# Low parts of 24 U chunks made ahead and kept in DRAM, and the rows of h2 and x1 in buffers of their own

## Chip, cores and metric

The kernel runs on one core of one Trainium2 chip. The metric is the device time of one execution in microseconds (us), as the median of several runs; a smaller number is better.

## What is computed

One decoder block on 512 tokens of width 1024, in float32. The first sub-layer mixes tokens (a gated MLP over positions, a windowed attention, two sigmoid branch gates, an output projection, a layer norm). The second, which takes two thirds of the time here, retrieves single-neuron experts:

```python
q = (xb @ w_pq).reshape(-1, PEER_HEADS, PEER_QDIM)          # xb: h2, the modulated x1
s1, s2 = keys1 . q1, keys2 . q2                             # 128 scores for each half of a head
v1, i1 = lax.top_k(s1, 16); v2, i2 = lax.top_k(s2, 16)
sc, ci = lax.top_k(v1[:, None] + v2[None, :], 16)           # 16 of 16384 experts, for each of 8 heads
g = jax.nn.softmax(sc)
act = gelu(einsum('thkd,td->thk', peer_u[e], xb))
out = einsum('thk,thkd->td', g * act, peer_v[e])
x = layer_norm(ALPHA * x + (1.0 + gt2) * out, ln2_g, ln2_b)
```

## The kernel before

**Numbers.** A float32 product is made of three TensorE products: each operand is split into a rounded high part (`hi`, a copy on ACT, ScalarE) and a low part (`lo = raw - hi`, on DVE, VectorE, or on POOL, GpSimd), and `mm3` (lines 57 to 65) runs hi x hi, hi x lo and lo x hi. A weight chunk of 128 x 1024 so costs one load of 512 KB, one ACT copy, one subtraction and the products.

**The first sub-layer** is staged as: modulation (`mod_chunk`, line 144: one 512 KB load `wa` and one DVE operation each), queries and attention, the gated MLP (`w_u`, then the position mixing into `aT`), then gate b and projection b in eight iterations (lines 341 to 350; each also does four `mod_chunk`), then gate a and projection a in eight iterations (lines 372 to 384), then the output projection and the layer norm (lines 387 to 429), which leave `xhat` (x1 before its gain and offset) and `h2T` (h2, transposed and split). `load_split` (line 112) loads and splits a weight chunk; its raw tiles and those of `mod_chunk` share one tag `raw` with 4 buffers.

**The experts.** The first three blocks of 128 tokens (384 tokens) are computed densely: all 16384 experts in 128 chunks of 128, U chunk (`h2T` by `peer_u`, 24 products of 384 columns) and V chunk (18 products of 512 columns into six accumulators). The last block of 128 tokens is computed by gathering: 128 rows of `peer_u` and 128 of `peer_v` for each token, through indirect DMAs on POOL's queue into the tag `rows` (4 buffers), each reduced by one DVE operation (`gather`, line 663). The order of stages:

- queries and scores (16 chunks of w_pq), while DVE finds the top 16s; U chunks follow while that lasts. In these stages the low parts are made by POOL (`last["pool"]`, line 455).
- spread (`spread`, line 606): the gates of 384 tokens are written out over all 16384 experts, in 24 groups of 16 tokens: for each, four DVE operations make one-hot tiles `oh`, TensorE multiplies them (32 products of 128 columns, f16), ACT copies the result to `stg`, and SP (SyncE) stores it to `Gd` in DRAM. Beside it run U chunks whose low parts DVE makes; 21 of them (NRES) stay in SBUF (`U_resident`, line 695) and are multiplied by the gates there; the others store their activations in `Ad`.
- rows (`rows_x1`, line 484): `h2n` (h2 of the last block, in natural layout, for the gather) and x1 out of `xhat`, in place, with rows loaded into the tag `raw` of `load_split2` (4 buffers).
- three more U chunks (VDLY), the 21 V chunks of the resident ones, then U and V chunks in pairs with the gather beside them ("pairs"), at last the V chunks of those whose activations went to `Ad` ("tail", loads `ar`), and the final layer norm.

**What sets the order.** The program is written as one sequence. Work that is to run beside other work is a list of generators, `bg`; `pump(us)` advances it by so many estimated microseconds per chunk. A planner then orders the instructions of each engine at compile time: an instruction goes where its engine is free and its operands are ready by the planner's own times, and among several that are ready the earlier one of the program goes first. On the chip each engine runs its instructions in that order, and one that waits holds up all behind it. `behind(a, b)` puts a after b on their engine.

## Time and profile before

| | us |
|---|---|
| median of 3 runs | 1731.55 (1729.62 to 1737.84) |
| the profiled execution | 1727.13 |
| its span, first to last instruction | 1725.4 |
| TensorE busy in it | 1667.5 (97%) |
| VectorE busy | 1346.7 (78%) |
| ScalarE busy | 685.6 (40%) |
| GpSimd busy | 474.2 (27%) |

A matmul counts as busy from its start to its modelled end, and several are in flight, so a busy TensorE need not be one at its full rate: the number of matmuls in a stretch tells more. In a table of stretches the granted clock (PEclk) is 1.00 at 2.4 GHz and 0.50 at 1.2 GHz; a value between is a mean of both over the stretch. The DMA share is the mean busy share of the core's 16 DMA engines. A row of such a table gives: stretch (us from the span's start), its length, then busy us and number of instructions (x) of PE (TensorE), PEld (its weight loads), DVE, ACT and POOL, then PEclk, DMA share and GB/s.

### The profile page before, as it was taken

The page shows a single profiled execution, that of the slowest core. Times are in us where ns is not written, and L with a number is a line of the kernel's source. Part 1 is how long each engine was busy: PE and PEld are TensorE (multiplying, and loading weights), DVE is VectorE, ACT ScalarE, POOL GpSimd, SP SyncE. Part 2 cuts the span into 40 slices and gives each one's busy share as a digit, 9 for nine tenths or more (in the row PEclk, how much of TensorE's full clock was granted, in tenths as well). Part 3 has the DMA queues.
Part 4 walks back from the last instruction along what each step waited for, and adds up shares of the span by engine and source line. Part 5 has one row for each costly group of instructions (what it writes and reads, how often), then busy time and mean ns, then how long its engine had stood idle before and what let it go on. Part 6 is the DMA issues. An engine that isn't in the chain of part 4 may idle for free.

```text
span 1725.4 us, 23595 instructions
## 1 busy us (share of the span) xinstructions
PE 1667.5 (97%) x8658; PEld 1440.2 (83%) x8658; DVE 1346.7 (78%) x2510; ACT 685.6 (40%) x1095; POOL 474.2 (27%) x333
## 2 busy tenths in 40 slices
PE   6999999999999999999999999999999999999997
PEld 3865778788788999999987789999999999988776
DVE  6467785554559999999988887878787888787687
ACT  3467632233333333455443233333333333343333
POOL 2000000000043455300014544434444545541102
PEclk9999999999999999999999999999999999999999
DMA  7502267642232355566599999999899899899973
GB/s 270 200 1 74 98 198 256 210 144 95 86 120 85 112 173 174 209 218 226 203 316 365 373 328 333 325 339 348 306 336 334 326 336 341 303 372 312 306 235 106
DMA packets 158695, 409.52 MB, mean 237 GB/s; under 512 B 19217, under 2 KB 66097, under 8 KB 158322
## 3 DMA queue, kind: packets, MB, share of 16 engines
q1 hardware_dynamic: 121186, 273.47, 46.2%
q0 software_dynamic: 36960, 134.50, 21.6%
q8 instruction: 68, 1.11, 0.3%
q14 instruction: 49, 0.40, 0.1%
q10 hardware_dynamic: 432, 0.04, 0.0%
HBM read 376.88 MB, written 30.82 MB: 236 GB/s over the span
## 4 chain that ended last, share of the span: by engine, by line
PE 52%; DVE 20%; issue 5%; DMA 4%; POOL 2%; ACT 1%; SPq 0%; DVEq 0%; POOLq 0%; ACTq 0%
PE acc L802 7%; PE acc L803 7%; PE acc L799 7%; PE psU L64 6%; PE psU L62 6%; PE psU L63 6%; POOL ru L669 2%; DMA ar<-Ad 2%; DMA wa<-in_w_ada_dram 2%; DVE oh L634 1%; DVE loU L458 1%; DVE oh L637 1%; DVE oh L633 1%; DVE oh L636 1%; DVE loV L458 1%
## 5 line engine op out<-in xcount | busy, mean ns | idle before, releaser
L62 PE MATMUL psU<-h2Thi,hiU 128*128 128x384 f32 x1008 | 340.9, 338 | 5.4 <-ACT hiU L450 3.7
L64 PE MATMUL psU<-h2Thi,loU 128*128 128x384 f32 x1008 | 340.4, 338 | 3.5 <-DVE loU L458 3.4
L63 PE MATMUL psU<-h2Tlo,hiU 128*128 128x384 f32 x1008 | 339.2, 337 | 0.0
L802 PE MATMUL acc<-loV,wh 128*128 128x512 f32 x768 | 301.5, 393 | 5.5 <-DVE loV L458 5.5
L803 PE MATMUL acc<-hiV,wl 128*128 128x512 f32 x768 | 300.5, 391 | 0.3 <-DVE wl L785 0.3
L799 PE MATMUL acc<-hiV,wh 128*128 128x512 f32 x768 | 298.8, 389 | 1.7 <-ACT wh L784 1.7
L669 POOL DMA_INDIRECT ru<-in_peer_u_dram,idx x128 | 157.2, 1228 | 368.6 <-DVE ru L673 351.5
L682 POOL DMA_INDIRECT rv<-in_peer_v_dram,idx x128 | 174.1, 1360 | 248.3 <-DVE facc L688 221.4
L458 DVE TENSOR_TENSOR loV<-rawV,hiV 128x1024 fp32r<-128x1024 f32 x128 | 156.3, 1222 | 90.3 <-ACT hiV L450 90.2
L450 ACT ACTIVATE hiV<-rawV 128x1024 fp32r<-128x1024 f32 x128 | 135.1, 1056 | 224.3 <-PE psU L63 188.6
L450 ACT ACTIVATE hiU<-rawU 128x1024 fp32r<-128x1024 f32 x126 | 133.9, 1062 | 216.6 <-POOL loU L456 68.0
L62 PEld LDWEIGHTS psU<-h2Thi,hiU 128*128 128x128 f32 x1008 | 190.5, 189 | 8.8 <-ACT hiU L450 3.9
L64 PEld LDWEIGHTS psU<-h2Thi,loU 128*128 128x128 f32 x1008 | 190.3, 189 | 5.3 <-DVE loU L458 5.2
L63 PEld LDWEIGHTS psU<-h2Tlo,hiU 128*128 128x128 f32 x1008 | 190.6, 189 | 2.6
L802 PEld LDWEIGHTS acc<-loV,wh 128*128 128x128 f32 x768 | 144.1, 188 | 39.5 <-DVE loV L458 10.9
L673 DVE SCALAR_TENSOR_TENSOR ru<-ru,h2n 128x1024 f32<-128x1024 f32 x128 | 154.4, 1220 | 24.3 <-DMA ru<-in_peer_u_dram,idx 24.1
L803 PEld LDWEIGHTS acc<-hiV,wl 128*128 128x128 f32 x768 | 144.1, 188 | 30.8 <-DVE wl L785 1.0
L799 PEld LDWEIGHTS acc<-hiV,wh 128*128 128x128 f32 x768 | 144.2, 188 | 30.5 <-ACT wh L784 2.0
L688 DVE SCALAR_TENSOR_TENSOR facc<-rv,wg,facc 128x1024 f32<-128x1024 f32 x126 | 159.4, 1279 | 11.4 <-DMA rv<-in_peer_v_dram,idx 11.4
L784 ACT ACTIVATE wh<-wf 128x384 fp32r<-128x384 f32 x107 | 56.1, 525 | 182.1 <-DVE wf L780 106.2
L456 POOL TENSOR_TENSOR lopq<-rawpq,hipq 128x1024 fp32r<-128x1024 f32 x16 | 39.0, 2445 | 322.2 <-ACT hipq L450 322.2
L458 DVE TENSOR_TENSOR loU<-rawU,hiU 128x1024 fp32r<-128x1024 f32 x96 | 116.9, 1218 | 2.8 <-ACT hiU L450 2.8
(629 smaller groups left out, 2929.4 us busy)
## 6 DMA issues: line engine op xcount, KB each, us to landing
rawU<-in_uT_dram SPq DMA_DIRECT2D x128, 512.0 KB, 4.2
rawV<-in_peer_v_dram SPq DMA_DIRECT2D x128, 512.0 KB, 6.2
wa<-in_w_ada_dram SPq DMA_DIRECT2D x48, 512.0 KB, 4.2
G<-Gd SPq DMA_DIRECT2D x11, 1536.0 KB, 14.8
Gd<-stg SPq DMA_DIRECT2D x24, 600.0 KB, 4.3
rawpq<-in_w_pq_dram SPq DMA_DIRECT2D x16, 512.0 KB, 3.6
Ad<-act SPq DMA_DIRECT2D x39, 192.0 KB, 2.2
ar<-Ad SPq DMA_DIRECT2D x9, 768.0 KB, 8.5
```

What stands on the lines that cost most here:

```text
L62: nc.tensor.matmul(ps, l.hi, r.hi, start=(i == 0), stop=False)
L63: nc.tensor.matmul(ps, l.hi, r.lo, start=False, stop=False)
L64: last = nc.tensor.matmul(ps, l.lo, r.hi, start=False, stop=(i == n - 1))
L450: h = nc.scalar.activation(hi, raw, AF.Copy)
L458: last["dve"] = nc.vector.tensor_sub(lo, raw, hi.bitcast(F32))
L669: d = nc.gpsimd.indirect_dma_start(out=rows, out_offset=None, in_=I["peer_u"], in_offset=bass.IndirectOffsetOnAxis(ap=idx[:, s:s + 1], axi ...
L673: paced(nc.vector.scalar_tensor_tensor(rows, rows, 1.0, h2n, op0=ALU.mult, op1=ALU.mult, accum_out=wg[:, s:s + 1]))
L682: nc.gpsimd.indirect_dma_start(out=rows, out_offset=None, in_=I["peer_v"], in_offset=bass.IndirectOffsetOnAxis(ap=idx[:, s:s + 1], axis=0))
L688: paced(nc.vector.scalar_tensor_tensor(fa, rows, wg[:, s:s + 1], fa, op0=ALU.mult, op1=ALU.add))
L799: m = nc.tensor.matmul(acc, l.hi, r.hi, start=st, stop=False)
L802: nc.tensor.matmul(acc, l.hi, r.lo, start=False, stop=False)
L803: nc.tensor.matmul(acc, l.lo, r.hi, start=False, stop=sp_)
```

## The change

Three parts:

1. The low parts of the last 24 U chunks (104 to 127) are made during the first sub-layer, in 48 halves of 128 x 512. For each half, POOL's queue loads 256 KB of `uT` into one of two buffers (tag `ht`, free by then), ACT copies it to a PSUM bank rounded (`hi`), DVE writes raw - hi in place, and POOL's queue stores it to a new DRAM tile `LoD`. The steps are written into the iterations of gate b (three in each) and of gate a (three in each); the first load is put behind the mask of the position mixing on POOL.
2. These 24 chunks are the first taken when the spread starts (`ready`): the 21 resident ones and three more. Their low part is loaded from `LoD` by SP (512 KB each), and DVE makes none. The U chunks 32 to 52, which were resident before, come among the pairs.
3. `rows_x1` is split: `rows_h2` is the first background work of the query stage and takes its rows into the tag `rows` of the gather; x1 is queued as background work at the start of the pairs, its two rows one after the other in the tag `facc1`.

```diff
+NPS = 24
+    LoD = dram.tile([NPS, P, D], F32, name="LoD")
+        def presplit():
+            raws = {}
+
+            def load(k):
+                raws[k] = wp.tile([P, S], F32, name=f"praw{k}", tag="ht", bufs=2)
+                d = nc.gpsimd.dma_start(raws[k], I["uT"][NCH - NPS + k // 2, :, (k % 2) * S:(k % 2 + 1) * S])
+                if k == 0:
+                    behind(d, mask)
+            load(0)
+            load(1)
+            for k in range(2 * NPS):
+                yield
+                hi = bank("po", 1, f"phi{k}").bitcast(F32R)
+                nc.scalar.activation(hi, raws[k], AF.Copy)
+                lo = raws[k].bitcast(F32R)
+                nc.vector.tensor_sub(lo, raws[k], hi.bitcast(F32))
+                nc.gpsimd.dma_start(LoD[k // 2, :, (k % 2) * S:(k % 2 + 1) * S], raws[k])
+                if k + 2 < 2 * NPS:
+                    load(k + 2)
+        ps_steps = presplit()
...
             for i in range(16 + 4 * j, 20 + 4 * j):
                 mod_chunk(i)
+                if i % 4 < 3:
+                    presplit_some(1)
...
             ps = proj_T(load_split(I["w_gate"][j], f"ga{j}"), hT, f"psga{j}")
+            presplit_some(2)
...
             ps = proj_T(load_split(I["w_pa"][j], f"pa{j}"), aT, f"pspa{j}")
+            presplit_some(1)
...
         wo[1] = load_split_wide(I["w_out"][1], "wo1", ("G", "H"))
+        presplit_some(100)
...
-    def load_split2(src, nm, pool=None):
+    def load_split2(src, nm, pool=None, low=None):
...
-        if last.get("pool"):
+        if low is not None:
+            nc.sync.dma_start(lo.bitcast(F32), low)
+        elif last.get("pool"):
...
-    def rows_x1():
-        g2r, b2r = raw_row("g2r"), raw_row("b2r")
+    def rows_h2():
+        g2r, b2r = (gat.tile([P, D], F32, name=nm, tag="rows", bufs=4) for nm in ("g2r", "b2r"))
...
-        g1, b1 = raw_row("g1"), raw_row("b1")
-        nc.sync.dma_start(g1, I["ln1r"][0].partition_broadcast(P))
-        nc.sync.dma_start(b1, I["ln1r"][1].partition_broadcast(P))
-        for t in range(NT):
-            nc.vector.tensor_mul(xhat[:, t, :], xhat[:, t, :], g1)
-            nc.vector.tensor_add(xhat[:, t, :], xhat[:, t, :], b1)
-            yield 2.4
+
+    def rows_x1():
+        for i, op in enumerate((ALU.mult, ALU.add)):
+            row = gat.tile([P, D], F32, name=f"ln1_{i}", tag="facc1", bufs=1)
+            nc.sync.dma_start(row, I["ln1r"][i].partition_broadcast(P))
+            for t in range(NT):
+                nc.vector.tensor_tensor(xhat[:, t, :], xhat[:, t, :], row, op=op)
+                yield 1.2
...
-        w = load_split2(I["uT"][i], f"U{i}")
+        w = load_split2(I["uT"][i], f"U{i}", low=LoD[i - NCH + NPS] if i >= NCH - NPS else None)
...
+    bg.append(rows_h2())
     qt = query(0, 0)
...
-        res["first"] = cur[0] + 1
+        res["first"] = NCH - NPS
...
-    bg += [topk_last(), softmax(), end_topk(), spread(), end_spread(), rows_x1()]
+    bg += [topk_last(), softmax(), end_topk(), spread(), end_spread()]
...
-    i = NPRE + 1
+    todo, ready = list(range(NPRE + 1, NCH - NPS)), list(range(NCH - NPS, NCH))
     while not done or len(res["ids"]) < NRES:
-        cur[0] = i
+        i = (ready if res and ready else todo).pop(0)
...
     for _ in range(VDLY):
+        i = (ready or todo).pop(0)
...
-    uvruns = runs(range(i, NCH))
+    todo += ready
+    uvruns = runs(todo)
...
     pend = None
+    bg.append(rows_x1())
...
-    for run in runs(spilled):
+    for run in runs(sorted(spilled)):
```

## Rows read from the trace of the kernel before

**Rows 1.** The page: each engine's busy us, share of the span, instructions.
```profile
PE 1667.5 (97%) x8658; PEld 1440.2 (83%) x8658; DVE 1346.7 (78%) x2510; ACT 685.6 (40%) x1095; POOL 474.2 (27%) x333
```

**Rows 2.** Table of stretches (columns above): spread, resident V chunks, pairs.
```profile
750.00:800.00 50.00, 49.76 (x449) 48.19 (x448) 50.00 (x63) 26.94 (x55) 0.00 (x0) 1.00 0.67 235
900.00:950.00 50.00, 48.09 (x206) 37.79 (x205) 40.45 (x61) 16.74 (x23) 22.50 (x19) 1.00 1.02 372
1050.00:1100.00 50.00, 50.00 (x254) 45.54 (x254) 40.75 (x61) 18.17 (x24) 21.93 (x19) 1.00 0.97 343
```

**Rows 3.** Timeline of TensorE in the spread: start us, us, engine, line, operation.
```profile
774.97 0.33 PE L62 MATMUL psU<-h2Thi,hiU 128*128 128x384 f32 x1
775.84 0.34 PE L64 MATMUL psU<-h2Thi,loU 128*128 128x384 f32 x1
776.21 0.23 PE L645 MATMUL psg<-oh,oh 128*128 128x128 f16 x1
778.01 0.22 PE L646 MATMUL psg<-oh,oh 128*128 128x128 f16 x1
```

**Rows 4.** Groups by line, 710 to 868 us: count, busy us, mean ns, idle before.
```profile
L62 PE MATMUL psU<-h2Thi,hiU 128*128 128x384 f32 x199 | 68.6, 345 | 1.7 <-ACT act L716 1.0 <-ACT act L706 0.7
L645 PE MATMUL psg<-oh,oh 128*128 128x128 f16 x368 | 44.9, 219 | 1.6 <-DVE oh L637 1.4
L458 DVE TENSOR_TENSOR loU<-rawU,hiU 128x1024 fp32r<-128x1024 f32 x25 | 30.3, 1214 | 0.7 <-ACT hiU L450 0.7
```

**Rows 5.** Stretches of 10 us: the spread's start, and the rows after its end.
```profile
710.00:720.00 10.00, 7.68 (x36) 7.17 (x35) 9.93 (x13) 4.41 (x7) 5.17 (x4) 0.83 0.86 318
870.00:880.00 10.00, 6.06 (x33) 5.38 (x31) 8.87 (x9) 5.49 (x10) 0.00 (x0) 0.67 0.84 285
```

**Rows 6.** Timelines of DVE and ACT at the spread's end.
```profile
867.61 1.21 DVE L489 TENSOR_TENSOR h2n<-xhat,g2r 128x1024 f32<-128x1024 f32 x1
...
873.57 1.06 ACT L450 ACTIVATE hiU<-rawU 128x1024 fp32r<-128x1024 f32 x1 [1.85 <-DMA rawU<-in_uT_dram]
```

**Rows 7.** Stretches of 10 us in gate b (the first has the stage's start).
```profile
260.00:270.00 10.00, 10.00 (x32) 7.99 (x33) 5.02 (x10) 1.34 (x2) 0.00 (x0) 0.71 0.79 262
290.00:300.00 10.00, 10.00 (x46) 8.29 (x45) 7.68 (x11) 2.56 (x3) 0.00 (x0) 1.00 0.68 231
```

**Rows 8.** Waits, whole span: total us, times, longest us.
```profile
DVE wf L780 <- DMA ar<-Ad: 32.9, 8, 5.4
DVE wa L147 <- DMA wa<-in_w_ada_dram: 32.0, 21, 3.3
```

**Rows 9.** DMA issues by line: queue, count, KB each, median us to landing.
```profile
rawU<-in_uT_dram SPq DMA_DIRECT2D x128, 512.0 KB, 4.2
...
Gd<-stg SPq DMA_DIRECT2D x24, 256.0 KB, 3.0
...
xr<-in_x_dram SPq DMA_DIRECT2D x8, 256.0 KB, 2.7
```

**Rows 10.** Timelines of POOL, ACT and DVE: two iterations of gate a, operations like presplit's.
```profile
57.98 0.76 POOL L206 DMA_DIRECT2D kd<-kd  x1 [23.53 <-ACT kd L204]
...
396.35 0.58 ACT L377 ACTIVATE ga<-psga 128x512 f32<-128x512 f32 x1
...
407.23 0.58 ACT L377 ACTIVATE ga<-psga 128x512 f32<-128x512 f32 x1
...
401.07 0.69 DVE L380 TENSOR_TENSOR mt<-pspa,ga 128x512 f32<-128x512 f32 x1 [3.37 <-PE pspa L64]
```

**Rows 11.** The mask on POOL (timeline), and the output projection's products (view of one tile).
```profile
203.39 1.59 POOL L314 TENSOR_SCALAR_AFFINE_SELECT wst<-wst 128x1024 f32<-128x1024 f32 x1 [109.39 <-DMA wst<-in_w_sp_dram]
...
L62 PE MATMUL pso<-wwhiwo,mThi x64: 389/389/395, 422.6 to 467.5; 128*128 128x512 f32 x64
```

**Rows 12.** Timeline of DVE at the start of the top 16s.
```profile
495.85 0.49 DVE L535 MAX8 v0h__3571<-sall 128x8 f32<-128x128 f32 x2 [11.94 <-ACT sall L532]
...
498.91 0.28 DVE L535 MAX8 v0l__5222<-sall 128x8 f32<-128x128 f32 x1
```

More of the change, by code (lines that the diff above doesn't have):

```diff
@@ L65, in mm3, with behind @@
         return last
+    def behind(ins, other):
+        tc.add_manual_dep(ins.ins, other.ins.name,
+                          mybir.DependencyInfo(mybir.DependencyClass.NoSync, mybir.DependencyReason.DATA))
     const = ctx.enter_context(tc.tile_pool(name="const", bufs=1, reuse_waits="tile"))
@@ L313, in block_kernel @@
         nc.sync.dma_start(wst, I["w_sp"])
-        nc.gpsimd.affine_select(wst, wst, pattern=[[0, 8], [1, P]], compare_op=ALU.is_ge, fill=0.0, base=0,
+        mask = nc.gpsimd.affine_select(wst, wst, pattern=[[0, 8], [1, P]], compare_op=ALU.is_ge, fill=0.0, base=0,
                                 channel_multiplier=-1)
@@ L338, in block_kernel, with presplit_some @@
         sp_.close()
+        def presplit():
[17 more added lines that the diff above has]
+        ps_steps = presplit()
+        def presplit_some(n):
+            for _ in range(n):
+                next(ps_steps, None)
         gp = fr.enter_context(tc.tile_pool(name="gp", bufs=1, reuse_waits="tile"))
@@ L435, in block_kernel @@
     last = {}
-    def behind(ins, other):
-        tc.add_manual_dep(ins.ins, other.ins.name,
-                          mybir.DependencyInfo(mybir.DependencyClass.NoSync, mybir.DependencyReason.DATA))
     def paced(ins):
         behind(ins, last["dve"])
-    def load_split2(src, nm, pool=None):
+    def load_split2(src, nm, pool=None, low=None):
         raw = pw.tile([P, NK * P], F32, name=f"raw{nm}", tag="raw", bufs=4)
@@ L477, in pump @@
                 bg.pop(0)
-    def raw_row(nm):
-        return pw.tile([P, D], F32, name=nm, tag="raw", bufs=4)
     h2n = gat.tile([P, D], F32, name="h2n", tag="facc0", bufs=1)
-    def rows_x1():
-        g2r, b2r = raw_row("g2r"), raw_row("b2r")
+    def rows_h2():
+        g2r, b2r = (gat.tile([P, D], F32, name=nm, tag="rows", bufs=4) for nm in ("g2r", "b2r"))
         nc.sync.dma_start(g2r, rowsD[2].partition_broadcast(P))
@@ L710, in U_chunk @@
     def U_chunk(i, keep_act):
-        w = load_split2(I["uT"][i], f"U{i}")
+        w = load_split2(I["uT"][i], f"U{i}", low=LoD[i - NCH + NPS] if i >= NCH - NPS else None)
         ps = pu.tile([P, SD], F32, name=f"psU{i}", tag="mm", bufs=2)
@@ L816, in block_kernel @@
     res = {}
-    cur = [NPRE]
     def end_topk():
@@ L867, in block_kernel @@
             pump(GPUMP if res else UPUMP + 1.2 * bool(last.get("pool")))
-        i += 1
     open_v()
     for _ in range(VDLY):
+        i = (ready or todo).pop(0)
         U_chunk(i, False)
@@ L873, in block_kernel @@
         pump(2.7)
-        i += 1
-    uvruns = runs(range(i, NCH))
+    todo += ready
+    uvruns = runs(todo)
     for n, j in enumerate(res["ids"]):
```

## The prediction

> **What bounds the kernel now.** I read the page first: TensorE is busy for 97% of the span [rows 1], so only a stretch in which TensorE falls short of its own rate can give time back. The table of stretches shows where that is, once matmuls are counted and not busy time. The rate comes from the timeline of the spread: two U products five apart start 0.87 us apart, 0.174 us each; 32 one-hot products start within 1.80 us, 0.058 us each [rows 3]. Two iterations of gate a, 48 products of 512 columns each, lie 10.88 us apart [rows 10], 0.227 us a product. A pair of a U and a V chunk then needs 24 x 0.174 + 18 x 0.227 = 8.26 us for 42 products, 254 in 50 us, and 254 is what the pairs reach [rows 2]. So the pairs are bound by TensorE and gain nothing from a freer DVE.
>
> The spread is not: DVE is busy there without a gap, 50.00 of 50 us [rows 2]. From 710 to 868 us it ran, among others, 25 subtractions loU of 1.21 us [rows 4]. But TensorE is close behind. It ran 595 U products there (199 of the kind shown, 198 of each of the two others) and 736 one-hot products (368 of each of two kinds) [rows 4]: 595 x 0.174 + 736 x 0.058 = 146 us of work in 158 us. **Only 12 us are lost in the spread**, 10 - 36 x 0.174 = 4 of them in its first 10 us, where the clock was at 1.2 GHz for a part (0.83), and the rest in small waits behind DVE. After its end come another 10 - 33 x 0.174 = 4 us, at a clock of 0.67 [rows 5]: the rows of h2 and x1 stand in DVE's order there (first at 867.61), their loads have taken raw buffers, and ACT waits for the next rawU until 873.57 [rows 6].
>
> **What the change removes.** First, 24 of the 25 subtractions of the spread, 24 x 1.21 = 29 us of DVE [rows 4]. DVE would need 158 - 29 = 129 us, TensorE 146: TensorE is late next. The pairs show that TensorE can run at its rate beside a busy DVE, but the start of the spread stays a chain through DVE (last top 16, softmax, first one-hots), so of its 4 us I leave 3: the spread gives **-9 us**, not -29. Ends: 0, if another wait takes its place, and -12, TensorE at its rate throughout.
> Second, ten row operations (1.21 us each [rows 6], 12 us of DVE) and four loads of 512 KB leave the end of the spread. The 4 us there shrink to what another boundary costs; I take **-4 us** (ends -5 and -2).
>
> **What it moves.** The h2 rows (two loads on SP, two DVE operations) go to the start of the query stage. There DVE has an idle stretch of 11.94 us before the first top 16 [rows 12], so 2.4 us are hidden; without that cover they would delay the top 16s by 2.4 us, during which DVE is full. The planner does pull work forward: an operation of the last block's top 16 (v0l), written after all heads, runs at 498.91, three microseconds after the first [rows 12]. The eight x1 operations depend on nothing but xhat and a free facc1 buffer, so they can go into the same gap; if they stay in the pairs, they meet a DVE that is busy 40.75 of 50 us [rows 2], 1.5 us free per pair, and need six or seven pairs. The second row's load waits on SP for the four multiplications, with rawU and rawV behind it; a raw buffer or two cover that. I take 0 for both, ends 0 and +4. By its pacing (2.4 estimated us less for the top 16s) one more U chunk falls into the stage before the spread: 40 chunks spilled instead of 39, 67 pairs instead of 68. TensorE's work is the same; the spilled list is now 0 to 36 and 125 to 127, six runs instead of five, 11 ar loads instead of 10. The waits for ar are 32.9 us in 8 [rows 8], 4 us each, some of it behind DVE's backlog: **+1.5 us** (ends 0 and +4).
>
> **What it adds in the spread.** 24 loads of 512 KB on SP, 12.6 MB, at 372 GB/s of full rate [rows 2] 34 us of all 16 engines. The spread's share of 0.67 [rows 2] is some 106 of 158 us; with the loads 140 of 149 us, 0.94. It fits, barely. A low part's buffer comes free when TensorE is done with the third chunk before, so its load has two chunks of 6 us each for a landing that now takes 4.2 [rows 9] and will take longer. **+2 us** (ends 0 and +9, the whole gain of the spread).
>
> **What it adds in the first sub-layer** is the term I know least, since no row shows a load, a split and a store in two buffers. One step by the nearest rows: ACT 0.58, DVE 0.69, an issue on POOL 0.76 [rows 10], the store landing 3.0, another issue 0.76, the load landing 2.7 [rows 9]: 8.5 us for a buffer, 4.2 us per step with two buffers; with 0.1 us for each of four handoffs (an estimate), 4.4. 48 steps need 211 us. The steps are written three to an iteration of 10.9 us: one in 3.6 us, 174 us in all. But the loads can start behind the mask, whose operation ends at 205 us, and the output projection's last products start at 467.5 [rows 11]: 262 us. So it fits if the planner spreads the steps by their real length. ACT and DVE have the time (28 and 33 us in all). DMA has not, in gate b: share 0.68 to 0.79 [rows 7]; DVE waits there for wa loads, 32.0 us in all, 21 times [rows 8], and the iterations just keep TensorE's rate (46 products begun or running in 10 us). Eight iterations take 87 us; 87 / 4.4 = 20 steps fall into gate b, 20 x 0.524 MB = 10.5 MB or 28 us at 372 GB/s on top of some 0.7 x 87 = 61: 89 of 87, saturated. A wa that lands 1 us later, with six raw loads per iteration through four buffers that are each used for about 7 us, costs 0 to 2 us of an iteration, and where TensorE falls idle the clock follows, as after 260 us, where it was 0.71 and 32 products were done instead of 46 [rows 7]. **+6 us**, between 0 (hidden by the slack) and +37 (below).
> The Trainium skill (DMA: Bandwidth & Descriptors, "Anatomy of one DMA") puts a DMA of this queue at 2.0 us plus its bytes over 436 GB/s. By that page 256 KB would take 2.6 us, and a step by estimate 4.2 instead of 4.4; the same formula would put rawU's 512 KB at 3.2 us where the row shows 4.2, so under load it is too low here, and I keep the rows.
>
> **The sum.** -9 - 4 + 0 + 1.5 + 2 + 6 = -3.5 us. The profiled execution took 1727.13 us, 1.7 above its span; it is 4.4 us under the median of the runs, which I take as the base: 1731.5 - 3.5 = **1728 us**. Half a per cent is 8.7 us, about what a measurement of this kernel can tell from no change.
>
> **The rivals.** (1) *The steps are hidden.* If the planner keeps wa ahead and the steps fill idle time, the front costs nothing and the spread's loads little: -12 - 5 + 1.5 = -15.5 at best, with the middle values -9 - 4 + 1.5 = -11.5, **1720 us**. For it: ACT's and DVE's idle time and the empty POOL queue in these stages. Against: the DMA share in gate b.
> (2) *The two buffers pace the front; slower than before.* If the planner takes a step for shorter than the chip does, it places the steps as densely as written, one in 3.6 us; each one then holds ACT, and all splits behind it, until its load has landed. It decides when a step really takes over 3.6 us where it was planned so: 3 x 4.4 = 13.2 us an iteration instead of 10.9, 16 x 2.3 = +37 us, so 1731.5 - 13 + 1.5 + 2 + 37 = **1759 us**; if only gate a, or half of the steps, are so, 1741. For it: in-order engines, and DVE's waits for wa, which show the order already runs into DMAs that land late. Against: a plan that starts at 205 us has 262 / 48 = 5.5 us for each step, and DVE and ACT have idle time in gate b (7.68 and 2.56 of 10 us busy [rows 7]).
> (3) *The spread becomes bound by DMA.* At a share of 0.94 the low parts land late and the 9 us do not come: 1731.5 - 4 + 1.5 + 6 = **1735 us**. For it: the resident V chunks, where the share is 1.02 and 206 products of mostly 512 columns (220 at the rate) are done in 50 us [rows 2]. Against: nearly everything in the spread is issued one or two chunks ahead.
> That the subtractions do not go away can't be: 24 chunks take their low part by load, and 25 run in the spread.
>
> **How the numbers follow.** The forecast with its neighbourhood, rival 3 included: 0.43, all within 8.7 us. Rival 1 and combinations beyond 8.7 us faster: 0.32. Rival 2, in whole or in part: 0.25. The range for 8 in 10 goes from 1716 (rival 1 at its best) to 1752 (two thirds of rival 2's price); beyond are the rest of rival 2 and a little below. By the same cases: faster by over 0.5% 0.32, within 0.5% 0.43, slower by over 0.5% 0.25.
>
> **What would show it.** In the profile after: no loU on DVE between the start of the spread and its end, DVE busy below 90% there, and some 146 us of products in about 150 us; the products per 10 us around the end of the spread at 55 or more, with the clock at 1.00. In the first sub-layer: 45 to 46 products per 10 us from 270 to 420 us if the steps are hidden, 38 and ACT waiting for the praw loads if rival 2 holds. The query stage starts later by what the front costs. For rival 3: TensorE or its weight loads waiting for a DMA of LoD, share above 0.95. The forecast is wrong if the output projection starts more than 15 us later than before (422.6 us [rows 11]), or if the spread does not get shorter by at least 5 us.

## The result, and the profile after

The changed kernel takes **1772.82 us** (median of 4, 1771.38 to 1777.24) against 1732.26 us (median of 4 runs of the kernel before): a ratio of **1.0244 [1.0223, 1.0265]** on record (these two medians by themselves give 1.0234): slower by a little over 2%. That is 45 us above the forecast and 21 us beyond the upper end of its range. All readings below are made between the two profiled executions, of 1773.86 and 1727.13 us: 46.7 us apart, 6 more than the medians, since the profiled execution of the kernel before is 5 us under its median.

The busy line of the page after, which answers to [rows 1]:

```profile
PE 1683.5 (95%) x8658; PEld 1446.0 (82%) x8658; DVE 1358.3 (77%) x2533; ACT 710.5 (40%) x1143; POOL 533.4 (30%) x430
```

TensorE has the same 8658 products; its busy time rose by 16 us, since single matmuls count as busy for longer (for pso up to 795 ns in the view below, 395 before; the median is 389 in both). Where the time went is read from the first products of four stages. The view of one tile, kernel after (line, engine, operation, count: min/median/max ns, first to last start in us); the line for pso answers to [rows 11]:

```profile
L63 PE MATMUL psgb<-hThi,whigb x64: 389/389/501, 234.2 to 356.2; 128*128 128x512 f32 x64
L63 PE MATMUL psga<-hThi,whiga x64: 387/389/499, 365.3 to 468.4; 128*128 128x512 f32 x64
L63 PE MATMUL pso<-wwhiwo,mThi x64: 389/389/795, 474.5 to 526.5; 128*128 128x512 f32 x64
L63 PE MATMUL psq<-h2Thi,hipq x128: 389/389/502, 541.3 to 640.8; 128*128 128x512 f32 x128
```

Gate b starts at 234 us, as before; then the stages fall back, to 52 us at the output projection and 58.5 us at the queries. Read in the same way for every kernel of this study (us from the first product of a stage to the first of the next; spread from its first to its last one-hot product, V from the first V product to the last):

| kernel | gate b | gate a | output projection, norm | queries and U | spread | to first V | V |
|---|---|---|---|---|---|---|---|
| before | 102.5 | 87.2 | 60.2 | 241.2 | 146.7 | 19.4 | 824.3 |
| **after** | **131.1** | **109.2** | **66.8** | **243.7** | **142.3** | **12.6** | **821.1** |
| e1, no steps after the first two | 94.3 | 87.2 | 61.2 | 248.2 | 142.2 | 12.7 | 819.2 |
| e2, transfers only | 125.9 | 87.2 | 61.2 | 248.4 | 142.2 | 12.7 | 822.1 |
| e3, engines' work only | 96.0 | 87.2 | 59.7 | 245.1 | 142.2 | 12.7 | 820.9 |
| e4, four buffers | 132.4 | 113.2 | 61.3 | 245.3 | 142.3 | 12.6 | 821.2 |
| e12, transfers of half the bytes | 118.1 | 87.2 | 62.4 | 248.5 | 142.2 | 12.6 | 822.9 |
| e14, transfers only, fifth raw buffer | 109.9 | 87.1 | 62.5 | 245.7 | 142.2 | 12.6 | 822.0 |
| e6, rows only | 102.0 | 87.1 | 59.8 | 247.8 | 146.9 | 12.4 | 821.0 |
| e5, 24 paced steps | 109.1 | 87.2 | 59.7 | 247.3 | 144.7 | 12.6 | 822.8 |
| e9, 24 paced steps after gate b | 102.9 | 87.2 | 67.5 | 246.4 | 144.6 | 12.7 | 818.3 |
| e10, 16 steps in gate a | 103.9 | 87.1 | 61.3 | 247.3 | 145.2 | 12.5 | 822.5 |
| e11, 2 early steps and 16 in gate a | 96.5 | 87.2 | 61.2 | 247.3 | 145.2 | 12.5 | 824.0 |
| e13, 2 early steps only | 94.3 | 87.1 | 59.7 | 248.5 | 148.4 | 12.4 | 825.5 |

One row against another: gate b +28.6, gate a +22.0, output projection +6.6, with 1.3 us ahead of gate b **+58.5 us in the front**; behind it +2.5 -4.4 -6.8 -3.2 = **-11.9 us**. V alone varies by some 3 us between kernels that have the same work there, so single differences of that size mean nothing. A row is one execution of its kernel, and not always a typical one: those of e4, e12 and e14 took 6.5, 6.2 and 4.5 us more than the medians of their kernels, those of e6 and of the kernel before 4.0 and 5.1 less.

What is late in gate a is plain in ScalarE's timeline. Kernel after, 13 us of gate a, about one iteration (start us, us, engine, line, operation, and in brackets the idle time before and what ended it):

```profile
386.90 0.60 ACT L361 ACTIVATE phi<-praw 128x512 fp32r<-128x512 f32 x1 [3.99 <-DMA praw<-in_uT_dram]
...
390.12 0.60 ACT L361 ACTIVATE phi<-praw 128x512 fp32r<-128x512 f32 x1 [2.06 <-DMA praw<-in_uT_dram]
390.65 1.04 ACT L126 ACTIVATE whiga<-rawga 128x1024 fp32r<-128x1024 f32 x1
391.60 0.58 ACT L413 ACTIVATE ga<-psga 128x512 f32<-128x512 f32 x1
396.55 0.60 ACT L361 ACTIVATE phi<-praw 128x512 fp32r<-128x512 f32 x1 [4.36 <-DMA praw<-in_uT_dram]
399.33 0.60 ACT L361 ACTIVATE phi<-praw 128x512 fp32r<-128x512 f32 x1 [2.18 <-DMA praw<-in_uT_dram]
399.86 1.04 ACT L126 ACTIVATE whipa<-rawpa 128x1024 fp32r<-128x1024 f32 x1
```

The phi copies stand in ScalarE's order ahead of whiga and whipa, the high parts of the next weights; each waits 2 to 4 us for its load, and the weights wait with it. The table of waits, kernel after, of the whole span (engine, line, what it waited for: us in total, times, longest us):

```profile
ACT phi L361 <- DMA praw<-in_uT_dram: 149.5, 41, 8.1
POOL LoD L364 <- DVE praw L363: 123.7, 39, 21.9
...
DVE praw L363 <- ACT phi L361: 98.7, 38, 5.6
POOL praw L353 <- DMA LoD<-praw: 97.4, 33, 7.1
```

It is a ring in which each waits for the next: the copy for the load, the subtraction for the copy, POOL's store for the subtraction, POOL's next load for the landing of the store. And TensorE at the end of it, in the waits of 234 to 365 us and of 365 to 474 us:

```profile
PE pspb L63 <- ACT whipb L126: 13.1, 4, 4.5
```
```profile
PE pspa L63 <- ACT whipa L126: 5.5, 3, 2.6
PE pspa L65 <- DVE wlopa L127: 5.4, 4, 2.1
```

Such a wait can be charged twice, where the granted clock falls with it: 18 products at 0.88, 18 and 26 at 0.66. It does not always (27 products at 1.00). Stretches of gate b and gate a, kernel after, which answer to [rows 7] (us, then busy time and count of PE, PEld, DVE, ACT and POOL, granted clock, DMA share, GB/s):

```profile
260.00:270.00 10.00, 10.00 (x46) 8.29 (x45) 9.55 (x15) 2.46 (x4) 1.09 (x2) 1.00 0.93 295
...
300.00:310.00 10.00, 5.29 (x18) 3.57 (x17) 4.62 (x6) 1.58 (x2) 1.81 (x4) 0.88 0.71 248
...
340.00:350.00 10.00, 6.67 (x18) 4.86 (x19) 5.65 (x8) 3.64 (x5) 2.19 (x4) 0.66 0.64 222
...
420.00:430.00 10.00, 6.96 (x27) 4.65 (x26) 4.10 (x7) 3.67 (x7) 2.20 (x4) 1.00 0.58 201
430.00:440.00 10.00, 8.87 (x26) 7.10 (x27) 4.22 (x6) 3.39 (x6) 2.20 (x4) 0.66 0.60 214
```

18 products in 10 us where 46 are the rate. In the two worst of these stretches the DMA share is 0.64 and 0.71: the transfers are being waited for, and the engines that make them are not full.

The spread went as hoped. Groups of the kernel after between its first and its last one-hot product, which answer to [rows 4], and two stretches in it, which answer to [rows 2]:

```profile
L63 PE MATMUL psU<-h2Thi,hiU 128*128 128x384 f32 x182 | 62.5, 343 | 0.0
...
L493 DVE TENSOR_TENSOR loU<-rawU,hiU 128x1024 fp32r<-128x1024 f32 x4 | 4.9, 1220 | 1.9 <-ACT hiU L483 1.9
```
```profile
800.00:850.00 50.00, 49.80 (x436) 48.48 (x435) 42.53 (x58) 27.38 (x57) 0.00 (x0) 1.00 0.88 312
850.00:900.00 50.00, 49.72 (x455) 48.26 (x455) 41.22 (x54) 28.28 (x58) 0.00 (x0) 1.00 0.84 306
```

4 subtractions are left (from 909.5 us on, in its last 18 us), DVE is busy for 82 to 85% of these stretches instead of all the time, and TensorE for 49.7 to 49.8 of 50 us. 547 U products (182 or 183 of each kind) at 0.174 and 768 one-hot products at 0.058 us make 139.7 us of work in 142.3. Around the spread's end 97 and 60 products per 10 us are done at a clock of 1.00 (920 to 940 us), where it was 33 at 0.67.

### The profile page after: what moved, and what is told of

It reads as the page before. It is cut to its first block, busy times and chain, and to the rows that moved or that the text cites. A ratio compares the mean times of both kernels' runs of the same rounds, so it can differ in the third digit from the quotient of the medians.

```text
span 1772.1 us, 23951 instructions
## 1 busy us (share of the span) xinstructions
PE 1683.5 (95%) x8658; PEld 1446.0 (82%) x8658; DVE 1358.3 (77%) x2533; ACT 710.5 (40%) x1143; POOL 533.4 (30%) x430
## 3 DMA queue, kind: packets, MB, share of 16 engines
q1 hardware_dynamic: 128018, 286.45, 46.7%
## 4 chain that ended last, share of the span: by engine, by line
PE 50%; DVE 18%; issue 15%; DMA 12%; POOL 3%; ACT 1%; SPq 0%; DVEq 0%; POOLq 0%; ACTq 0%
PE acc L835 8%; PE acc L836 8%; PE acc L832 7%; PE psU L65 5%; PE psU L63 5%; PE psU L64 5%; DMA praw<-in_uT_dram 5%; DMA LoD<-praw 3%; POOL ru L702 2%; DMA ar<-Ad 1%; PE pss L253 1%; DMA ru<-in_peer_u_dram,idx 1%; PE psgv L63 1%; PE psgv L65 1%; PE psgv L64 1%
## 5 line engine op out<-in xcount | busy, mean ns | idle before, releaser
L363 DVE TENSOR_TENSOR praw<-praw,phi 128x512 fp32r<-128x512 f32 x48 | 32.9, 685 | 98.8 <-ACT phi L361 98.7
L491 POOL TENSOR_TENSOR loU<-rawU,hiU 128x1024 fp32r<-128x1024 f32 x31 | 76.6, 2470 | 61.4 <-ACT hiU L483 61.4
```

## The experiments

Three theories were to be told apart. **A**: the steps' transfers take DMA time from the weights of gate b. **B**: a step holds ScalarE's in-order queue until its load has landed. **C** (rival 2 of the prediction in its narrow form): the two buffers set the pace, and more of them would help. The recorded expectations have letters of their own: A1 in them is B here, A2 is A, A3 that the engines' own work costs time; from e4 on C there is A and B together, and D is C here.

**e1, no steps after the first two.** Against the change (all 24 chunks then load the first one's low part, so the loads of the spread stay):

```diff
-            for k in range(2 * NPS):
+            for k in range(2):
-                if k + 2 < 2 * NPS:
+                if k + 2 < 2:
...
-        w = load_split2(I["uT"][i], f"U{i}", low=LoD[i - NCH + NPS] if i >= NCH - NPS else None)
+        w = load_split2(I["uT"][i], f"U{i}", low=LoD[0] if i >= NCH - NPS else None)
```

> The change without 46 of the 48 presplit steps: only halves 0 and 1 are loaded, split and stored, and the 24 ready chunks all load this one low part (so 23 chunks are multiplied by the low part of another: that part of the computation is left out). All of the query, spread and pairs stages is as in the change. Theory A (the steps in the gate stages cost all that was lost, the later stages gain): the output projection starts within 3 us of 422.6 us and the time is 14 us below before, 1714 to 1722 us. Theory B (the later stages lose too, by loads of low parts that share the DMA engines): 1728 to 1735 us.

Measured 1710.91 us, 0.9877 [0.986, 0.9893], 3 us under the expected range. So the 46 later steps cost 62 us, all of it in the front: gate b 94.3 instead of 131.1, gate a 87.2 instead of 109.2. It also did something that no theory had: its gate b is 8 us shorter than that of the kernel before (e13 below).

**e2, transfers only**, and **e3, engines' work only.** e2 leaves the copy and the subtraction out of each step, so that raw halves are stored:

```diff
-                hi = bank("po", 1, f"phi{k}").bitcast(F32R)
-                nc.scalar.activation(hi, raws[k], AF.Copy)
-                lo = raws[k].bitcast(F32R)
-                nc.vector.tensor_sub(lo, raws[k], hi.bitcast(F32))
```

e3 keeps these and leaves out the loads and stores of all steps but the first two:

```diff
+                raws[k] = raws.get(k - 2)
+                if k >= 2:
+                    return
...
-                nc.gpsimd.dma_start(LoD[k // 2, :, (k % 2) * S:(k % 2 + 1) * S], raws[k])
+                if k < 2:
+                    nc.gpsimd.dma_start(LoD[k // 2, :, (k % 2) * S:(k % 2 + 1) * S], raws[k])
```

> All 48 steps of the change with their loads and stores in the same two buffers on POOL's queue, but without the ACT copy and the DVE subtraction: what is stored as the low part is the raw chunk (the low parts of 24 chunks are left out). Theory A1 (ACT and DVE wait in order for each half's load; the traffic does not matter): the gate stages keep TensorE's rate, the output projection starts at 423 to 430 us, time 1716 to 1724. Theory A2 (DMA bandwidth in gate b: wa, gb and pb land late because of 25 MB more): the output projection still starts at 450 us or later, time above 1745.

> All 48 ACT copies and DVE subtractions of the change at their places, on two buffers that are loaded and stored once each (the low parts of 23 chunks are left out), without the other 46 loads and 46 stores. Theory A1 (the wait for transfers is the cost, ACT's 28 us and DVE's 33 us are hidden): output projection at 423 to 430 us, time 1716 to 1726. Theory A3 (ACT and DVE are late by their own work, as DVE is full before gate b): output projection 10 to 30 us later than before, time 1730 to 1750.

Measured: e2 1748.62 us, 1.0097 [1.008, 1.0114]; e3 1710.32 us, 0.9876 [0.9859, 0.9892], 6 us under its range. The work of ACT and DVE costs nothing at all. The transfers by themselves cost 38 us against e1, 31.6 of them in gate b and **none in gate a**, not even 21 loads there in 87.1 us (e14 below; the change has 24 in 109.2). The remaining 24 us of the 62 need both, a copy in ScalarE's order that waits for a transfer: 22.0 of them are gate a. So B holds in gate a, and in gate b A alone is enough for most of a loss of that size. That the change loses its 36.8 us there by A isn't shown: nothing holds e2's ring, and 24 of its loads were issued in gate b, 18 of the change's. The waits of VectorE for wa in gate b, in e1, in e2 and in the change, and the copies' in the change:

```profile
DVE wa L154 <- DMA wa<-in_w_ada_dram: 15.3, 13, 3.1
```
```profile
DVE wa L154 <- DMA wa<-in_w_ada_dram: 45.5, 20, 4.6
```
```profile
ACT phi L361 <- DMA praw<-in_uT_dram: 78.6, 18, 8.1
...
DVE praw L363 <- ACT phi L361: 40.9, 15, 5.4
...
DVE wa L154 <- DMA wa<-in_w_ada_dram: 4.7, 5, 1.8
```

In e2 VectorE waits for late wa loads. In the change it waits behind the copies and comes to wa when that has landed, so there the trace points to B in gate b too; a run with the change's transfers, and copies that do not wait for them, would be needed to part the two.

**e4, four buffers.** The raw halves in two more buffers (those of `hf`), and loads four steps ahead:

```diff
-                raws[k] = wp.tile([P, S], F32, name=f"praw{k}", tag="ht", bufs=2)
+                raws[k] = (wp if k % 4 < 2 else gp).tile([P, S], F32, name=f"praw{k}", tag="ht" if k % 4 < 2 else "hf", bufs=2)
...
-                if k + 2 < 2 * NPS:
-                    load(k + 2)
+                if k + 4 < 2 * NPS:
+                    load(k + 4)
```

> The whole change with four buffers for the halves instead of two (the two more are those of hf, which nothing else uses before the output projection), and each load four steps ahead. After the runs before, the front's loss of 62 us is split: 32 us in gate b by the transfers alone, the rest by ACT waiting for a half's load. Theory C (both hold): gate a recovers its rate, gate b stays 30 us late, output projection at 440 to 455 us, time 1738 to 1752. Theory D (the two buffers alone pace the front): output projection at 425 us or earlier, time below 1725. If four buffers fill the DMA engines more: gate b is even later, time above 1765.

Measured 1767.42 us, 1.0203 [1.0181, 1.0225], in the third of the expected ranges, but not by a later gate b: gate b 132.4, gate a 113.2. Twice the buffers give nothing in either gate, so C in its narrow form is wrong. The steps themselves did run faster: 26 copies fall into gate b instead of 19, the last one is at 433.8 us instead of 479.6, and behind it gate a runs at 45 to 46 products per 10 us. Up to there gate a loses as much with fewer but denser steps (20 copies). Its waits, whole span:

```profile
POOL praw L353 <- DMA LoD<-praw: 109.6, 34, 6.4
...
ACT phi L361 <- DMA praw<-in_uT_dram: 81.9, 26, 6.4
```

The copies still wait for loads. A likely reason is POOL's queue, which is in order too: a load that reuses a buffer waits there for the landing of the store that empties it, and the stores behind that load wait with it. No run put loads and stores on different queues, so this reason is argued and not shown.

**e12, half the bytes.** e2 with 128 KB instead of 256 KB in each load and store after the first two steps (`n_(k)` is S for these two and S // 2 for the others; the store is shown, the load is cut in the same way):

```diff
-                nc.gpsimd.dma_start(LoD[k // 2, :, (k % 2) * S:(k % 2 + 1) * S], raws[k])
+                nc.gpsimd.dma_start(LoD[k // 2, :, (k % 2) * S:(k % 2) * S + n_(k)], raws[k][:, 0:n_(k)])
```

> The transfers of the change without the work of ScalarE and VectorE on them, as in the kernel with the transfers alone, but after the first two steps each load and each store carries half the bytes (128 KB, not 256 KB); the number and the place of the transfers are the same. The low parts of 23 chunks are left out: the spread loads one stored chunk for all 24, in its full size. With whole transfers the stretch from the first product of gate b to the first of gate a grew from 94 to 126 us. If the bytes are what costs (the DMA engines have no room left in gate b), about half of these 32 us stays: gate b of 106 to 114 us and a time of 1728 to 1736 us. If it is the number of transfers or their fixed time, 120 us or more and about 1746 us. If the room left is as large as the bytes that are now asked for, under 100 us and about 1715 us.

Measured 1735.14 us, 1.0008 [0.9988, 1.0027]; gate b 118.1 in the profiled execution. This does not decide between bytes and number. By the medians 24 of e2's 38 us stay, 64%; by gate b 23.8 of 31.6 us, 75%, but that execution took 1741.33 us, the longest of ten (1725.77 to 1741.33). The number was not the same either: smaller steps run faster, and 28 loads fall into gate b where e2 has 24, so 58% of the bytes are left there and not 50%. What suffers is the same loop in both: VectorE waits in gate b for wa for 38.5 us in e12, 45.5 in e2 and 15.3 in e1, and the rest of the stage is 79.6, 80.4 and 79.0 us, nearly the same in all three.

**e14, a fifth raw buffer** for the weights and wa that SP loads, in e2 (xr and hf, used later, give the room):

```diff
-            raw = wp.tile([P, NK * P], F32, name=f"raw{nm}", tag="raw", bufs=4)
+            raw = wp.tile([P, NK * P], F32, name=f"raw{nm}", tag="raw", bufs=5)
...
-            wa = wp.tile([P, D], F32, name=f"wa{j}", tag="raw", bufs=4)
+            wa = wp.tile([P, D], F32, name=f"wa{j}", tag="raw", bufs=5)
```

> The transfers of the change without the work of ScalarE and VectorE on them (so the low parts of 24 chunks are left out), as in the kernel with the transfers alone, with five buffers in place of four for the weights that SyncE loads in the front; the room comes from xr and hf, which have one buffer each and are used at the output projection only. Read at gate b, from its first product to the first of gate a: 125.9 us with four buffers, 94.3 us without the transfers, 118.1 us with half the bytes. If gate b is slow because each of SyncE's loads lands later and only four are under way at a time, the fifth buffer gives back up to a fifth of the cycle: 102 to 112 us. If the DMA engines have no room left, five loads under way land later still and it stays at 122 to 128 us.

Measured 1726.28 us, 0.9969 [0.9956, 0.9981], 22 us less than e2; **gate b 109.9 instead of 125.9**, as expected: half of what the transfers cost there comes back, with 20 loads in it (one in 5.5 us; e2 24, one in 5.2). Stretches of e2, then of e14 (columns as above):

```profile
300.00:310.00 10.00, 7.19 (x31) 5.56 (x31) 5.07 (x8) 2.02 (x3) 2.19 (x4) 0.99 0.85 273
320.00:330.00 10.00, 7.88 (x34) 5.87 (x32) 6.25 (x11) 1.54 (x2) 1.84 (x4) 1.00 0.92 319
```
```profile
270.00:280.00 10.00, 9.52 (x42) 7.62 (x41) 6.14 (x10) 2.60 (x3) 1.65 (x3) 1.00 0.96 350
300.00:310.00 10.00, 9.72 (x36) 7.88 (x37) 4.50 (x7) 1.06 (x1) 1.71 (x4) 0.83 0.97 360
```

and landings, 230 to 350 us, of the kernel before and then of e14 (queue, count, KB each, median us to landing):

```profile
wa<-in_w_ada_dram SPq DMA_DIRECT2D x26, 512.0 KB, 3.8
```
```profile
wa<-in_w_ada_dram SPq DMA_DIRECT2D x27, 512.0 KB, 6.6
praw<-in_uT_dram POOLq DMA_DIRECT2D x22, 256.0 KB, 5.7
```

From 260 to 340 us e2, with four buffers, moved 301 GB/s in the mean (273 to 319) at a share of 0.87; e14, with five, 335 (286 to 360) at 0.94. So there was some room in the DMA engines; gate b could not use it. Its weights are a closed loop of four buffers, and what counts is how long the loop waits: VectorE's wait for wa is 25.1 us in e14 and 45.5 in e2, though where landings are recorded wa takes 6.6 us in e14 instead of 3.8 before, since one load more is under way. The median landing alone does not tell: e13 below has 4.5 us for wa, more than e12's 4.4, and loses nothing in gate b. At a share of 0.94 little room is left, and 15.6 us of the 31.6 stay.

**e6, rows only**: the kernel before with the rows of h2 and x1 out of the raw buffers, and no low parts ahead (`presplit` and its calls, and `low=`, are left out of the change).

> The kernel before with part 3 of the change alone: rows of h2 at the query stage in the gather's buffers, rows of x1 in facc1 at the pairs; no low parts are made ahead. By the sum of the prediction -4 us at the spread's end and 0 to +4 elsewhere: 1726 to 1732 us. If the 6.8 us that the stretch between spread and first V chunk got shorter in the change all come from the rows: 1724 to 1726. If they come from the missing subtractions of the three chunks there: no change, 1731 to 1733.

Measured 1726.43 us, 0.9968 [0.9954, 0.9982]: 6 us. The end of the spread gives 7.0 (12.4 us to the first V instead of 19.4); what the other stages gain and lose nearly cancels.

**e5, 24 paced steps.** Every second chunk of the 24, and each copy held behind the sigmoid or the mT copy of its own stretch, so that the planner can't put steps closer: 8 written into gate b, 16 into gate a (7 and 15 copies ran there). The core of it:

```diff
-                nc.scalar.activation(hi, raws[k], AF.Copy)
+                p = nc.scalar.activation(hi, raws[k], AF.Copy)
+                if pace:
+                    behind(p, pace[0])
...
-            nc.scalar.activation(gt, ps, AF.Sigmoid)
+            presplit_some(1, nc.scalar.activation(gt, ps, AF.Sigmoid))
```

**e9** moves the 8 steps of gate b to the output projection (each behind the `z` product there), **e10** leaves them out (8 chunks, 16 steps, all in gate a).

> Low parts of 12 of the 24 ready chunks only (every other one; DVE makes the others in the spread), 24 steps, each put behind ACT's own work of its place: one step per iteration in gate b, two in gate a, the rest at the output projection. Theory C: no wait of ACT for praw worth naming, gate b late by the share of transfers that fall into it (8 of 24 to 30 that did): 5 to 10 us; time 1718 to 1726. Theory D: the front as without steps, 1710 to 1716. If DVE's 12 subtractions in the spread cost as much as 24: 5 us more in either.

> As the half version, but no step in gate b: 16 steps in gate a, one for each group of 24 products, and 8 at the output projection. Theory C: no transfers beside wa, so gate b as without steps, gate a at TensorE's rate; output projection at 414 to 424 us, time 1709 to 1718. If transfers in gate a do hurt through ACT after all: output projection above 430 us.

> The change with the low parts of only 8 chunks (every second one of the last 24) made ahead: 16 steps of half a chunk, one for each group of 24 products of the gates of the second half of the projections, none in the first half (gate b) and none at the output projection; the other 16 chunks are split in the spread as before. Theory: a step costs time where the room of the DMA engines is used up (gate b) or where it stands ahead of urgent work of ScalarE (output projection); in gate a, one step per 24 products costs nothing. So the queries start where the kernel with the rows alone starts them (481.5 us, within 2 us), the rest takes 1222 to 1226 us from there, and the time is 1720 to 1726 us. Rival (every step costs something wherever it stands, about 62 us / 48 = 1.3 us each): 1726.4 + 16 x 1.3 - 4 = 1743 us.

Measured: e5 1731.14 us, 0.9996 [0.9983, 1.0009]; e9 1729.52 us, 0.9989 [0.9977, 1.0001]; e10 1726.77 us, 0.9962 [0.9946, 0.9977]: above the expected ranges, e5 by 5 us, e9 by 11.5, e10 by 1. In all three gate a runs at TensorE's rate (87.1 to 87.2 us) with 14 or 15 copies in it: one step in 6 us, in the right place, costs nothing there. At the output projection steps are dear, for there ScalarE is on the way to h2. e9 has 10 copies there; the stretch ahead of its queries, and the copies' waits from 423 to 490 us:

```profile
470.00:480.00 10.00, 5.35 (x21) 4.54 (x21) 4.09 (x9) 4.92 (x13) 0.92 (x3) 0.83 0.65 259
```
```profile
ACT phi L361 <- DMA praw<-in_uT_dram: 23.3, 7, 4.8
```

67.5 us instead of e6's 59.8. In gate b they are dear as well: e5's 7 copies there, one in 16 us, make it 109.1 us against 102.0 to 103.9 in e6, e9 and e10, which have none. e10 has no cost that can be told from noise and no gain either: 0.9962 against 0.9968 for the rows alone. Eight chunks shorten the spread by 1.7 us (145.2 against 146.9), twelve by 2.3, the full 24 by 4.6.

**e11, two early steps and 16 in gate a**, and **e13, two early steps only** (one chunk). Steps 0 and 1 stand where the change has them; against e10:

```diff
+                if 16 <= i < 19:
+                    presplit_some(1)
+            if j == NK - 1:
+                pace[:] = [g_]
+                presplit_some(1)
```

> As the kernel with 8 chunks, but 9 chunks: the first two steps (half a chunk each) stand where the change puts them, early in gate b, and the other 16 are paced, one for each group of 24 products, in gate a. The kernels that had just the first two steps in gate b started the output projection at 414.6 to 416.0 us, the kernel before at 422.6 us, since the stall of TensorE between 250 and 270 us is missing in them. If that stall goes with the order that the two early steps bring about, the output projection starts near 415 us, the queries near 475 us, and the time is 1711 to 1716 us, faster than both kernels. If the stall went for another reason, the output projection starts near 422 us and the time is 1720 to 1726 us.

> As the kernel with 9 chunks, of which only the first is kept: the two early steps of the change (one chunk of low parts), the rows and the order of the chunks; the other 23 chunks are split in the spread as before. If the gain of the two early steps is the order that the planner finds for gate b, and the low parts themselves bring only what the spread shows, the output projection starts at 414 to 417 us, the spread is 146 to 147 us long as with the rows alone, and the time is 1716 to 1722 us: as fast as with 9 chunks, within 3 us. If the low parts of the other 8 chunks were what made the kernel with 9 chunks faster, the time is that of the rows alone, about 1726 us, or above.

Measured: e11 **1720.64 us, 0.9918 [0.99, 0.9936]**; e13 **1719.7 us, 0.9923 [0.9906, 0.9939]**. Both beat the kernel before by 12 us and the change by 52, and they are equal: eight chunks more are worth nothing. Their spread is 3.2 us shorter, but gate b is 2.2, the output projection 1.5 and the end behind the last V product 2.8 us longer (13.3 instead of 10.5). Their output projections start at 416.4 and 415.1 us, as expected if the order is what counts; e11's time is 5 us above what I expected then, and e13's spread is 1.4 us longer than expected. What the order is, ScalarE's and TensorE's timelines show, before (first fence) and e13 (second):

```profile
256.30 1.06 ACT L119 ACTIVATE whigb<-rawgb 128x1024 fp32r<-128x1024 f32 x1 [2.61 <-PE psgb L63]
257.26 0.61 ACT L336 ACTIVATE aThi<-mx 128x512 fp32r<-128x512 f32 x1
257.89 1.28 ACT L346 ACT_TABLE_LOAD   x1
259.19 1.09 ACT L346 ACTIVATE gb<-psgb 128x512 f32<-128x512 f32 x2
```
```profile
253.92 1.28 ACT L393 ACT_TABLE_LOAD   x1
255.21 0.60 ACT L393 ACTIVATE gb<-psgb 128x512 f32<-128x512 f32 x1
257.24 1.06 ACT L127 ACTIVATE whigb<-rawgb 128x1024 fp32r<-128x1024 f32 x1 [1.43 <-issue]
```

Before, the first sigmoid of gate b (with the load of its table) waits in ScalarE's order behind the next whigb, which itself waits 2.61 us for TensorE, and the last aThi copy; the aThi copies alternate singly with DVE. In e13 the planner has put these in pairs, and the sigmoid 4 us earlier and ahead of that whigb. TensorE before, and the stretches before and of e13:

```profile
259.84 0.80 PE L62 MATMUL pspb<-oThi,whipb 128*128 128x512 f32 x1 [3.40 <-ACT gb L346]
```
```profile
250.00:260.00 10.00, 6.60 (x30) 5.17 (x28) 9.71 (x15) 6.00 (x8) 0.00 (x0) 0.95 0.60 208
```
```profile
250.00:260.00 10.00, 10.00 (x46) 8.29 (x45) 10.00 (x17) 5.53 (x7) 0.00 (x0) 1.00 0.65 211
260.00:270.00 10.00, 10.00 (x46) 8.29 (x45) 7.32 (x11) 2.61 (x3) 0.00 (x0) 1.00 0.88 305
```

Before, a wait of 3.40 us for that sigmoid, and behind it 10 us at a clock of 0.71 with 32 products [rows 7]; in e13 46 and 46. The 30 products that are missing before, 16 and 14, at 0.227 us, are 6.8 of the 8.2 us by which e13's gate b is shorter. But e6 has the same late sigmoid and the same wait of 3.40 us, and no loss of clock behind it (45 products from 260 to 270 us at 1.00), and still takes 102.0 us for gate b, with products lost later in the stage; so what the sigmoid costs by itself isn't shown, only what the order does. That two added steps bring this order about is how the planner's choice fell here; why it fell so was not looked into.

## Why the prediction was wrong

**The front, +6 predicted, +58.5 measured, is the step that failed.** It had three terms.

*The length of a step* was right: 4.4 us estimated; in gate a 24 steps stand between 365.3 and 474.5 us, 4.55 us each. In gate b 19 steps took 131.1 us, 6.9 each, where load and store land later than the rows of a quieter stretch let expect: 5.7 us for 256 KB in e14 (the change's own landings are not recorded) against 2.7 and 3.0 [rows 9]. The Trainium skill (DMA: Bandwidth & Descriptors, "Anatomy of one DMA") would have it 2.6 us, by an estimate from its figures, further off. The prediction was right to prefer the rows, but they were from the wrong stage.

*The plan.* The prediction let the steps spread over 262 us, "if the planner spreads the steps by their real length", and priced the other case, three steps to an iteration with ScalarE held at each, as rival 2 with a chance of 0.25. The trace has that case: three phi to an iteration of gate a, 13.65 us long, where rival 2 said 13.2. Its price for gate a was 8 x 2.3 = 18 us; 22.0 came. So rival 2 was the right mechanism in gate a and nearly the right size. Its argument against ("a plan that starts at 205 us has 5.5 us for each step") took an average over the front for the plan. The steps are written inside the iterations that the planner lays out, and only 4 of 48 copies ran before gate b. A static order that puts an operation waiting for a DMA ahead of weights should have carried more than a quarter.

*Gate b's transfers.* Here the prediction had the right sum (89 of 87 us of DMA time, "saturated") and wrote +6 beside it; rival 2 gave gate b the 18 us of ScalarE's waits and nothing for the transfers. They cost 31.6 us by themselves (e2 against e1), and together with ScalarE's waits 36.8. The size was missed because room was counted in bytes at 372 GB/s. What mattered was that gate b's weights come through four raw buffers, a loop that a fifth buffer relieved by 16 us while the traffic stayed. The prediction names that loop ("six raw loads per iteration through four buffers") and then takes 0 to 2 us of an iteration for a landing 1 us later; wa landed 2.8 us later in e14, and e2's gate b lost 31.6 / 8 = 4 us of an iteration. The two costs overlap in gate b: three steps at gate a's pace would make 13.65 us an iteration, the loop alone makes 15.7 (e2, whose transfers come closer together), and 16.4 came. How much of the change's loss there is the loop's and how much the copies' stays open; its own waits are the copies' (78.6 us, against 4.7 for wa). Against the kernel before the loss is 28.6 and not 36.8 us only because the change also has the better order of e1 and e13 there (8.2 us). Rival 2's 1759 us was too low for all this: the front's 58.5 us are its 36.8 and 21.7 that it left out, 1.3 ahead of gate b, 10.2 in it, 3.6 in gate a, and 6.6 at the output projection, where the last two copies (474.1 and 479.6 us) and stores stand in front of the norm's work.

Two smaller readings of the prediction were off, without weight for its failure: the 32.0 us in 21 waits for wa are those of the whole span, 24.0 in 17 of them in gate b; and 1752 us, called two thirds of rival 2's price, is four fifths by its own sum (two thirds give 1747).

**Behind the front, -9.5 predicted, -11.9 measured**; the terms were right in sign but for one.
- Spread: -9 predicted, -4.4 measured (-4.7 in e1 against the rows alone). The mechanism was right, TensorE is late next, at 98% of its rate. The size was off because the window of 710 to 868 us had 14 us ahead of the first one-hot product at 724.0; in the spread itself, 724.0 to 870.7, only 146.7 - 139.4 = 7 us were lost.
- Its end: -4 predicted with ends -5 and -2; 19.4 us to the first V became 12.4 to 12.7 in all kernels with the moved rows: -7.
- Moved rows, 0 (to +4): the stage of the queries grew by 2.5 us (6.6 in e6), of which the one U chunk that the prediction moved there is 24 x 0.174 = 4.2. In e6 that leaves 2.4 us, the very length of the two h2 operations, but other kernels differ by as much, so it isn't shown.
- V, +1.5: it is 3.2 us shorter, of which that chunk is more than the whole.
- LoD's loads in the spread, +2, and rival 3: no wait of TensorE for them is on the trace; the share is 0.84 to 0.88, not 0.94, at 306 to 312 GB/s. Rival 3 is out.
- Rival 1 (the steps are hidden, 1720 us) is what e11 comes to with 18 steps of 48, and there not by the low parts.

Of the signs that the prediction named, the ones for rival 2 came: the output projection 52 us later (15 was the limit), 18 to 41 products per 10 us in gate b from 270 us on and 26 to 46 in gate a, ScalarE waiting for praw. The spread had to get 5 us shorter and got 4.4.

**Not settled**: how much of the 6.6 us at the output projection is the two late steps alone (e4 has 61.3 there with all 48 steps), what parts the two costs in gate b, whether bytes or number of the transfers set the first of them, and whether a planner that knew the real length of a step would place 48 of them at no cost.

## What to carry to other kernels

An engine with idle time is not room for a step that begins with a DMA: in a static order the step holds everything behind it until its load has landed, so count the wait, not the 0.6 us of work, and place one step per stretch that is longer than the step's whole ring. A stage whose operands come through a few reused buffers can lose to added transfers before the DMA engines are full, as gate b did at a share of 0.87; look for a queue that waits for buffers at every load and for the engine that waits for these loads, and price added traffic by that wait. And when two kernels differ by an edit that should do nothing (here two early steps), look where the order changed: 8 us of gate b lay in it.

## What the runs showed that was not expected

- With four raw buffers gate b moved 301 GB/s in the mean at a DMA share of 0.87 (e2, 260 to 340 us); with a fifth 335 GB/s at 0.94 (e14), and the stage fell from 125.9 to 109.9 us. A share of 0.87 was also that of e13 where gate b lost nothing (298 GB/s, 260 to 320 us), so the share does not tell whether a stage waits.
- With 21 loads and 22 stores of 256 KB in 87.1 us, gate a of e14 kept TensorE's rate at 251 GB/s; with 24 copies that wait for such loads the change's gate a took 109.2 us at 215 GB/s.
- Doubling the buffers of a load, split and store ring made its steps run faster (the last copy at 433.8 instead of 479.6 us) and gained nothing for the stages they stand in (gate b 131.1 to 132.4, gate a 109.2 to 113.2 us).
- A wait of 3.40 us on TensorE was followed by 10 us at the lower clock level before (a mean granted clock of 0.71, so partly at 1.2 instead of 2.4 GHz; 32 products instead of 46), and in e6 the same wait by 10 us at 1.00 with 45 products.
